# Pairing units product by product around a change of operands, and streaming the residual through DRAM, in a Strassen down projection

## The chip, the cores and the metric

The kernel runs on one core of a Trainium2 chip. The metric is the device time of one execution in microseconds (us), measured on the chip; the time before is the median of three runs. Beside the timed runs there is one profiled execution, whose trace gives the busy times, waits and transfers shown below. TensorE multiplies matrices, VectorE and ScalarE work element by element, SyncE (SP) and GpSimd (POOL) issue most of the DMA transfers.

## The reference

The reference is one inference step of a decoder layer, in float32, for a prompt of 512 tokens and 8 single decode tokens, which the kernel handles together as 520 columns. With D = 2048 and FF = 8192:

```
x = x + mixer(rmsnorm(x))                 # RG-LRU and mLSTM groups, projections w_in and w_out
x = x + cross_attn(rmsnorm(x), mk, mv)    # w_cq, w_mk, w_mv, w_co; 256 memory tokens
x = x + relu(rmsnorm(x) @ w_up)**2 @ w_down
y = rmsnorm(x) * g_final
```

It returns y for both kinds of tokens, the recurrent states, the convolution states, and the memory keys and values. The change is in the last matrix product, `@ w_down` (8192 x 2048), and in the helper that all the large products share.

## The kernel before

**Layout.** Activations lie transposed: 128 features on the partitions, 520 tokens in the free dimension, in two halves of 260 (`HT`). A float32 matrix is split into a high part and a low part, both in the fp32r type, and each product is three matmuls: high by high, high by low, low by high.

**Strassen products.** `strassen(key, n, ...)` computes a projection in `n` units of 256 output features. A unit is one level of Strassen's scheme in Winograd's form: seven products instead of eight. One product is 24 matmuls of 128 x 128 weights by 128 x 260 activations, accumulated in one PSUM bank; `ORDER` (L781) says for each product which of the three accumulators a, b, c it uses and which of the eight stored combinations of the activation blocks (a "slot") it reads. Accumulator a takes four of the seven products of a unit, c two, b one. `w_out`, `w_cq` and `w_co` have 8 units, `w_up` has 32. The 8192 rows of `w_down` are cut into four quarters, d0 to d3 (`NG = 4`), each with 8 units over the same 2048 outputs.

**Weights.** A unit reads four weight blocks of 128 x 1024 (A11, A21, A22, A12), fetched by `fetch` on SP's queue into a ring of seven tiles (`praw`, tag "raw"). `weights` (L877) forms the Strassen sums of the blocks on VectorE (L819), with one more tile of the ring for the running sum. `split_weights` (L97) makes the high part on ScalarE (L100) and the low part on VectorE (L101). In the main loop (L1428) weights are prepared two products ahead (`LOOK = 2`) and at a higher priority. A unit of the Strassen kind fetches the four blocks of the next unit during its first four products; the "plain" stages (keys and values of the memory) work in groups of four jobs, each with one weight block, and do the same.

**Operand sets.** For each projection the activations stand in DRAM as eight combinations (`td[key]`). Seven of them are in use, each as two batches of a high and a low tile: 28 tiles in the pool `ops`, all of its room. `set_load` (L848) loads one set: two transfers of 520 KB on SP's queue (L843), a cast on ScalarE (L844) and a subtraction on VectorE (L839) for each. A set of the next projection can be loaded only when the last unit of the current one has run the product that reads the old set in its place: `leave` is called after each product of the last unit. This happens between up and d0 and between the quarters of down.

**Evacuation.** After a product, `up_evac` copies or adds the accumulator into a tile t; after the seventh it squares the rectified result into w, forms the combinations and stores them to DRAM by POOL's queue (`spill`, L830). In down, `onto` (L927) adds the accumulator to the residual x on VectorE (L931). The residual is 16 tiles of 128 x 520, loaded at the start of d0 by `down_enter` (L1319) and kept in SBUF to the end, where `final` normalises and stores it.

**Order.** Pools and tiles come from a planner. It orders instructions by a priority, which follows the order of the program except that weights and evacuations are raised, and places the waits. Each engine and each DMA queue then works through its instructions in the planned order. `enter` closes the pools of a stage and opens those of the next in the same memory; a tile there waits for the tiles that held its place.

## Time and profile before

| | before |
|---|---|
| median of three runs | 2822.25 us |
| lowest and highest run | 2814.14 and 2824.98 us |
| the profiled execution, device time | 2829.93 us |
| its span, first to last instruction | 2828.2 us |
| TensorE busy | 2696.4 us, 95% |
| VectorE busy | 2265.6 us, 80% |
| ScalarE busy | 1389.7 us, 49% |
| moved by DMA | 525.67 MB, mean 186 GB/s |
| mean granted TensorE clock | 0.979 |

Up runs from about 1410 us of the span to about 2100, down from there to 2802. "Busy" is the time in which at least one instruction of an engine runs; matmuls overlap, so a busy TensorE need not be at its peak. The granted clock is the share of full speed that TensorE had. A line such as L839 is a line of the kernel, often in a helper that several stages use; then the names of the tiles tell the stage: op is an operand set, raw and raws are weight blocks, whi and wlo their high and low part, x the residual, acca, accb and accc the accumulators, tdd the DRAM copy of the operands of down. In a row of waits stand who waited and for whom, the total in us, how often, and the longest. In a row of windows stand the stretch in us, its length, the busy time of each engine with its number of instructions, the granted clock, the mean share of the DMA engines, and GB/s.

### The profile page before, as it was taken

To read this page: it belongs to the slowest core of one execution; us is meant where nothing else is said; L and a number is where in the kernel's file an instruction comes from. 1 tells how busy PE (TensorE), PEld (TensorE's weight loads), DVE (VectorE), ACT (ScalarE), POOL (GpSimd) and SP (SyncE) were. 2 spreads that over 40 slices of the span, in tenths; PEclk is the share of its full clock that TensorE was granted. 3 is DMA by queue.
4 is the path that set the end of the run, shared out by engine and by line. 5 is a ranking of instruction groups with operands and counts; after the bars stand their busy time and mean duration, and the time that the engine had idled before them with its cause. 6 is when DMAs were issued, how large, how long until landed. Compare 5 with 4: busy or idle time off the path is not lost.

```text
span 2828.2 us, 51905 instructions
## 1 busy us (share of the span) xinstructions
PE 2696.4 (95%) x21122; PEld 2613.9 (92%) x21122; DVE 2265.6 (80%) x3453; ACT 1389.7 (49%) x1857; POOL 93.9 (3%) x138
## 2 busy tenths in 40 slices
PE   8999999999999999989989999999999989999996
PEld 7999999999999997669979999999999989999896
DVE  7777787758888888789888777777787787887986
ACT  5455556535455444445464555555554343433543
POOL 0000000120000000000001000000000000000000
PEclk9999999999999999989999999999999999999998
DMA  4666542378677467985667454545465353533532
GB/s 167 191 216 212 191 151 91 115 272 271 203 260 261 158 197 282 328 300 188 207 214 262 150 166 150 166 150 165 150 210 203 105 191 102 172 126 112 191 107 82
DMA packets 173095, 525.67 MB, mean 186 GB/s; under 512 B 23084, under 2 KB 33004, under 8 KB 172856
## 3 DMA queue, kind: packets, MB, share of 16 engines
q1 hardware_dynamic: 151080, 442.50, 46.7%
q0 software_dynamic: 20624, 77.72, 7.8%
q8 instruction: 166, 2.72, 0.4%
q10 hardware_dynamic: 1152, 2.13, 0.2%
q14 instruction: 73, 0.60, 0.1%
HBM read 414.67 MB, written 107.73 MB: 185 GB/s over the span
## 4 chain that ended last, share of the span: by engine, by line
PE 74%; DVE 8%; DMA 7%; issue 7%; ACT 3%; POOL 0%; SPq 0%; DVEq 0%; POOLq 0%; ACTq 0%
PE acca L924 29%; PE accc L924 14%; PE mm L165 13%; PE accb L924 7%; PE mv L1159 3%; DVE wlo L101 2%; DVE op L839 2%; PE mk L1139 2%; PE ax L184 2%; DMA op<-tdd 2%; PE row L1086 1%; ACT whi L100 1%; DMA x<-dx 1%; PE aux L184 1%; ACT op L844 1%
## 5 line engine op out<-in xcount | busy, mean ns | idle before, releaser
L924 PE MATMUL acca<-op,whi 128*128 128x260 f32 x5632 | 1045.2, 285 | 37.9 <-DVE op L839 13.9
L924 PEld LDWEIGHTS acca<-op,whi 128*128 128x128 f32 x5632 | 876.6, 190 | 46.2 <-DVE op L839 17.7
L924 PE MATMUL acca<-op,wlo 128*128 128x260 f32 x2816 | 800.9, 284 | 4.5 <-DVE wlo L101 4.5
L100 ACT CAST whi<-raw 128x1024 fp32r<-128x1024 f32 x416 | 435.7, 1050 | 479.3 <-PE acca L924 155.2
L101 DVE TENSOR_TENSOR wlo<-raw,whi 128x1024 fp32r<-128x1024 f32 x416 | 506.8, 1220 | 73.7 <-ACT whi L100 69.0
L924 PEld LDWEIGHTS acca<-op,wlo 128*128 128x128 f32 x2816 | 534.5, 190 | 5.5 <-DVE wlo L101 5.2
L924 PE MATMUL accc<-op,whi 128*128 128x260 f32 x2816 | 523.2, 284 | 3.4 <-DVE op L839 1.8
L100 ACT CAST whi<-raws 128x1024 fp32r<-128x1024 f32 x264 | 276.8, 1049 | 399.7 <-PE accc L924 141.0
L165 PE MATMUL mm<-xa,whi 128*128 128x260 f32 x2624 | 433.3, 287 | 13.6 <-ACT whi L100 9.2
L924 PEld LDWEIGHTS accc<-op,whi 128*128 128x128 f32 x2816 | 437.0, 189 | 7.1 <-DVE op L839 2.9
L101 DVE TENSOR_TENSOR wlo<-raws,whi 128x1024 fp32r<-128x1024 f32 x264 | 322.5, 1222 | 124.7 <-ACT whi L100 124.2
L924 PE MATMUL accc<-op,wlo 128*128 128x260 f32 x1408 | 398.0, 283 | 0.0
L165 PEld LDWEIGHTS mm<-xa,whi 128*128 128x128 f32 x2624 | 367.4, 191 | 15.2 <-ACT whi L100 9.2
L924 PE MATMUL accb<-op,whi 128*128 128x260 f32 x1408 | 262.1, 285 | 15.6 <-DVE op L839 8.7
L165 PE MATMUL mm<-xa,wlo 128*128 128x260 f32 x1312 | 269.6, 287 | 0.0
L924 PEld LDWEIGHTS accc<-op,wlo 128*128 128x128 f32 x1408 | 266.4, 189 | 0.0
L924 PEld LDWEIGHTS accb<-op,whi 128*128 128x128 f32 x1408 | 218.2, 189 | 19.1 <-DVE op L839 11.0
L165 PEld LDWEIGHTS mm<-xa,wlo 128*128 128x128 f32 x1312 | 204.9, 191 | 0.5 <-DVE wlo L101 0.3
L924 PE MATMUL accb<-op,wlo 128*128 128x260 f32 x704 | 198.9, 282 | 0.0
L839 DVE TENSOR_TENSOR op<-op,op 128x1040 fp32r<-128x1040 f32 (+3 forms) x136 | 160.0, 1178 | 35.5 <-ACT op L844 26.3
L844 ACT CAST op<-op 128x1040 fp32r<-128x1040 f32 (+1 forms) x112 | 112.4, 1006 | 96.4 <-DMA op<-tdd 54.8
L100 ACT CAST whi<-wraw 128x1024 fp32r<-128x1024 f32 x82 | 85.6, 1044 | 142.9 <-PE mm L165 119.6
(367 smaller groups left out, 3232.0 us busy)
## 6 DMA issues: line engine op xcount, KB each, us to landing
raw<-in_w_up SPq DMA_DIRECT2D x128, 512.0 KB, 3.5
raw<-in_w_down SPq DMA_DIRECT2D x128, 512.0 KB, 3.5
wraw<-in_w_in SPq DMA_DIRECT2D x80, 512.0 KB, 4.5
tdd<-w POOLq DMA_DIRECT2D x32, 1040.0 KB, 6.3
op<-tdd SPq DMA_DIRECT2D x56, 520.0 KB, 5.5
raw<-in_w_mk SPq DMA_DIRECT2D x32, 512.0 KB, 5.1
raw<-in_w_out SPq DMA_DIRECT2D x32, 512.0 KB, 3.9
raw<-in_w_cq SPq DMA_DIRECT2D x32, 512.0 KB, 3.7
```

Of the source, the lines that this page charges most:

```text
L100: S.copy(hi, raw)
L101: V.tensor_tensor(out=lo, in0=raw, in1=hi.bitcast(F32), op=ALU.subtract)
L165: PE.matmul(ps[:, hf, 0:HT], w[:, j, :], x[:, HALF[hf]], start=(k == 0 and wi == 0), stop=(k == n - 1 and wi == 2))
L184: PE.matmul(out, u, v, start=first and i == 0, stop=last and i == 2)
L839: V.tensor_tensor(out=lo, in0=src, in1=hi.bitcast(F32), op=ALU.subtract)
L844: S.copy(hi[:, 0:n], lo[:, 0:n].bitcast(F32))
L924: PE.matmul(out, u[:, k], x[:, j], start=(new and k == 0 and i == 0), stop=(k == 7 and i == 2), skip_group_check=not new)
L1086: PE.matmul(ps, identr[0:NB, b:b + 1].to_broadcast([NB, P]), r, start=i == 0, stop=i == 1)
L1139: PE.matmul(st["mk"], u[:, i, :], x, start=(k == 0 and wi == 0), stop=(k == KB - 1 and wi == 2))
L1159: PE.matmul(st["mv"][i], x[:, ms], u[:, j], start=(k == 0 and wi == 0), stop=(k == KB - 1 and wi == 2))
```

## The change

The units around a change of operands run in pairs. `strassen` gets `pairs`: the first units of pairs. A pair runs product 0 of both units, then product 1 of both, and so on, so that both use the same operand set in turn. In d0, d1 and d2 units 0 and 1 and units 6 and 7 are pairs, in d3 units 0 and 1; up has none. The weights of the second unit of a pair (`seconds`) do not use the ring `praw`, but a pool y of four tiles, or tiles of the residual's pool in d3. Both units of a pair hold an accumulator a at the same time; there are two.

The main loop no longer fetches by the position in the unit before. Each weight block is fetched a fixed number of jobs before the job that first needs it (`NEED`): seven in a Strassen stage, four in a plain one.

The residual is no longer resident. `down_load(u)` loads the 128 x 1040 tile of unit u; in the first three quarters it is stored back to DRAM by POOL's queue after the unit's last product, with four tiles in the pool x; in d3 there are eight tiles and nothing is stored, so that `final` finds all of them. The loads are hung on products of earlier units (`hooks`, run at the end of a job). The pools of down are opened in the last unit of up, after its t and w have been allocated.

```diff
+YROW = 1154
...
             def go():
                 if "stack" in stage:
                     stage["stack"].close()
+                stage.clear()
                 stage["stack"] = ExitStack()
...
+        seconds = set()
+
         def fetch(k, q):
-            if k < len(sources):
+            if k not in seconds:
                 t = praw.tile([P, 8, P], F32, tag="raw", name=nm("raw"))
-                load(t, sources[k][q])
-                raws[k, q] = t
+            else:
+                n = "y" if "y" in stage else "x"
+                t = stage[n].tile([P, YROW] if n == "y" else [P, 2 * T], F32, tag=n, name=nm("rawp"))
+                t = t[:, 0:1024].rearrange("p (a b) -> p a b", b=P)
+            load(t, sources[k][q])
+            raws[k, q] = t
...
-        def strassen(key, n, src, evac, enter_=None, leave=None, left=None):
-
+        def strassen(key, n, src, evac, enter_=None, leave=None, left=None, pairs=(), hooks={}):
+            order = []
             for u in range(n):
-                k = len(sources)
-                sources.append([src(u, i, j) for i, j in ((0, 0), (1, 0), (1, 1), (0, 1))])
-                box = {}
-                for p in range(7):
-                    job = dict(unit=k, q=p, cost=0.3, prep=lambda k=k, p=p: weights(k, p),
...
+                if u in pairs:
+                    order += [(v, p) for p in range(7) for v in (u, u + 1)]
+                elif u - 1 not in pairs:
+                    order += [(u, p) for p in range(7)]
+            base, boxes = len(sources), [{} for _ in range(n)]
+            sources.extend([src(u, i, j) for i, j in ((0, 0), (1, 0), (1, 1), (0, 1))] for u in range(n))
+            seconds.update(base + u + 1 for u in pairs)
+            for u, p in order:
+                k, box = base + u, boxes[u]
+                job = dict(unit=k, q=p, kind=1, cost=0.3, prep=lambda k=k, p=p: weights(k, p),
...
+                if (u, p) in hooks:
+                    job["hook"] = hooks[u, p]
+                seq.append(job)
...
         def up_enter():
-            enter("d", t=2, w=2, x=2, r=1)()
+            enter("d", x=2, r=1, t=2, w=2)()
             start(scale_back())
...
         def up_evac(u, p, box):
             t = blocks(box, p)
+            if u == UP - 1 and p == 0:
+                box["w"] = tl("w", (P, 8, HT))
+                enter("e", y=4, x=4)()
             if p == 6:
-                w = tl("w", (P, 8, HT))
+                w = box.pop("w", None) or tl("w", (P, 8, HT))
...
-        def down_enter():
-            enter("e", x=16, ss=1)()
-            for m in range(KB):
-                X.append(tl("x", (P, T)))
-                load(X[m], dx[3][m // 2][:, m % 2])
+        def down_load(u):
+            x = tl("x", (P, 2 * T))
+            x = x.rearrange("p (i t) -> p i t", i=2)
+            load(x, dx[3][u])
+            X.append(x[:, 0])
+            X.append(x[:, 1])
+            st["X", u] = x
 
         def down_evac(u, p, box, last):
-            onto(X[2 * u:2 * u + 2], p, box["out"])
+            onto([st["X", u][:, 0], st["X", u][:, 1]], p, box["out"])
+            if p == 6 and not last:
+                store(dx[3][u], st["X", u])
...
-        strassen("up", UP, sq_src("w_up"), up_evac, up_enter, lambda s: set_load("d0", s))
+        strassen("up", UP, sq_src("w_up"), up_evac, up_enter, lambda s: set_load("d0", s),
+                 hooks={(UP - 1, 3): lambda: (down_load(0), down_load(1))})
+
+        def down_hooks(g):
+            last = g == NG - 1
+            hooks = {(1, 4): lambda: down_load(2)}
+            for u in range(2, 5):
+                hooks[u, 3] = lambda u=u: down_load(u + 1)
+            if last:
+                for u in (5, 6):
+                    hooks[u, 3] = lambda u=u: down_load(u + 1)
+            else:
+                hooks[5, 3] = lambda: (down_load(6), down_load(7))
+                if g == NG - 2:
+                    hooks[7, 3] = lambda: (enter("f", x=8, ss=1)(), X.clear())
+                    hooks[7, 5] = lambda: (down_load(0), down_load(1))
+                else:
+                    hooks[7, 3] = lambda: (down_load(0), down_load(1))
+            return hooks
+
         for g in range(NG):
+            last = g == NG - 1
             strassen(f"d{g}", 8, lambda u, i, j, g=g: a["w_down"][2 * u + i, g, j],
-                     lambda u, p, box, g=g: down_evac(u, p, box, g == NG - 1),
-                     down_enter if g == 0 else None,
-                     (lambda s, g=g: set_load(f"d{g + 1}", s)) if g < NG - 1 else None)
+                     lambda u, p, box, last=last: down_evac(u, p, box, last),
+                     leave=None if last else lambda s, g=g: set_load(f"d{g + 1}", s),
+                     pairs=(0,) if last else (0, 6),
+                     hooks=down_hooks(g))
...
-        for q in range(4):
-            fetch(0, q)
+        NEED = (0, 1, 1, 3)
+        fetches = [[] for _ in seq]
+        for n, j in enumerate(seq):
+            for i in range(4):
+                if j["q"] == (NEED[i] if j["kind"] else i):
+                    at = n - (7 if j["kind"] else 4)
+                    fetches[max(at, 0)].append((j["unit"], i, at < 0))
...
             with tc.high_priority(offset=AHEAD):
-                if j["q"] < 4:
-                    fetch(j["unit"] + 1, j["q"])
+                for k, i, early_ in fetches[n]:
+                    if not early_:
+                        fetch(k, i)
                 prep(n + LOOK)
...
+            if "hook" in j:
+                j["hook"]()
```

More of the change, by code (lines that the diff above doesn't have):

```diff
@@ L891, in weights @@
             return R((A11, SS, SS, A12, A21, SS, A22)[p])
[L893 removed]
+        def strassen(key, n, src, evac, enter_=None, leave=None, left=None, pairs=(), hooks={}):
+            order = []
             for u in range(n):
[L896 to L910 removed]
+                if u in pairs:
[8 more added lines that the diff above has]
+                job = dict(unit=k, q=p, kind=1, cost=0.3, prep=lambda k=k, p=p: weights(k, p),
+                           run=lambda w, p=p, box=box: product(key, p, w, box),
+                           post=lambda u=u, p=p, box=box: evac(u, p, box))
+                if u == 0 and p == 0 and enter_:
+                    job["enter"] = enter_
+                if u == n - 1:
+                    if leave:
+                        job["after"] = lambda p=p: leave(ORDER[p][2])
+                    if p == 6 and left:
+                        job["after"] = lambda p=p: (leave and leave(ORDER[p][2]), left())
+                if (u, p) in hooks:
+                    job["hook"] = hooks[u, p]
+                seq.append(job)
@@ L1374, in plain @@
                 for q in range(4):
-                    seq.append(dict(unit=k, q=q, cost=1.5, prep=lambda k=k, q=q: raws[k, q],
+                    seq.append(dict(unit=k, q=q, kind=0, cost=1.5, prep=lambda k=k, q=q: raws[k, q],
                                     run=lambda w, g=q0 + q: run(g, w), post=lambda g=q0 + q: post(g)))
@@ L1421, in rest @@
                 mem_load(k4, store)
-        for q in range(4):
-            fetch(0, q)
+        NEED = (0, 1, 1, 3)
[5 more added lines that the diff above has]
+                    fetches[max(at, 0)].append((j["unit"], i, at < 0))
+        for k, i, early_ in list(fetches[0]):
+            if early_:
+                fetch(k, i)
         for n in range(LOOK):
```

11 lines of the change are left out of this document (1 added, 10 removed).

## The prediction

> **What bounds the kernel now.** I read the page first, then the windows, the chain of waits, and the timelines of single engines, each time from a quiet stretch of the down projection to a change of operands.
>
> ```profile
> span 2828.2 us, 51905 instructions
> PE 2696.4 (95%) x21122; PEld 2613.9 (92%) x21122; DVE 2265.6 (80%) x3453; ACT 1389.7 (49%) x1857; POOL 93.9 (3%) x138
> ```
>
> TensorE is busy for 95% of the span, so only the rest, and matmuls at a lowered clock, can be won. Where does it lose time in down? The windows (us of the stretch, then busy time and instructions of each engine, clock, DMA share, GB/s) show a stretch inside a quarter, then the changes into the first, second and fourth quarter:
>
> ```profile
> 2145.00:2255.00 110.00, 110.00 (x916) 109.92 (x915) 88.93 (x102) 40.90 (x40) 0.00 (x0) 1.00 0.33 106
> 2080.00:2145.00 65.00, 53.35 (x410) 52.11 (x409) 52.08 (x57) 36.33 (x40) 1.70 (x2) 0.89 0.81 291
> 2255.00:2320.00 65.00, 57.65 (x436) 55.33 (x436) 52.70 (x58) 32.03 (x32) 0.00 (x0) 0.95 0.54 196
> 2605.00:2670.00 65.00, 58.63 (x469) 56.67 (x468) 56.82 (x65) 35.12 (x37) 0.00 (x0) 1.00 0.56 203
> ```
>
> Inside a quarter TensorE never stops. At the changes it idles 11.65, 7.35 and 6.37 us. What a change costs in all comes from the chain of waits (start, us, what): "x48" on acca is the last product of a unit followed by the first of the next, so it marks unit boundaries (x35 is the same piece cut short).
>
> ```profile
> 2082.71 5.77 PE acca L924 x48
> 2159.36 5.77 PE acca L924 x48
> 2179.56 5.77 PE acca L924 x48
> 2260.39 5.77 PE acca L924 x48
> 2333.81 5.77 PE acca L924 x48
> 2434.84 4.23 PE acca L924 x35
> 2507.94 5.77 PE acca L924 x48
> 2608.97 4.23 PE acca L924 x35
> 2678.50 5.77 PE acca L924 x48
> ```
>
> A quiet unit lasts 2179.56 - 2159.36 = 20.2 us, a product 2.887 us; 2159.36 to 2260.39 is five units without loss. Across each change lie three units (60.6 us), and the clock shows 76.65, 73.42, 73.10 and 69.53 us. So the changes cost 16.0, 12.8, 12.5 and 8.9 us: **50.2 us in all, the most that can be won here.**
>
> What is late in a change? The waits of TensorE at the first change, then VectorE back to back in the second (start, us, line, tile):
>
> ```profile
> PE acca L924 <- DVE x L931: 5.1, 1, 5.1
> PE accb L924 <- ACT op L844: 4.3, 1, 4.3
> PE accb L924 <- DVE op L839: 2.3, 2, 1.7
> ```
> ```profile
> 2289.85 1.22 DVE L101 TENSOR_TENSOR wlo<-raws,whi 128x1024 fp32r<-128x1024 f32 x1
> 2290.99 1.22 DVE L101 TENSOR_TENSOR wlo<-raw,whi 128x1024 fp32r<-128x1024 f32 x1
> 2292.12 0.42 DVE L931 TENSOR_TENSOR x<-accc,x 128x260 f32<-128x260 f32 x1
> 2292.46 1.22 DVE L101 TENSOR_TENSOR wlo<-raw,whi 128x1024 fp32r<-128x1024 f32 x1
> 2293.59 1.23 DVE L839 TENSOR_TENSOR op<-op,op 128x1040 fp32r<-128x1040 f32 x1
> 2294.74 0.42 DVE L931 TENSOR_TENSOR x<-acca,x 128x260 f32<-128x260 f32 x1
> ```
>
> When it never waits, VectorE starts a weight split (L101) every 1.14 us, a residual add (L931) every 0.34, an operand conversion (L839) every 1.15; the Strassen sums (L819, group row below) last as long as the splits. A unit has 7 splits, 7 adds and 4 sums: 14.9 us, **2.13 us per product of 2.887**.
>
> ```profile
> L819 DVE TENSOR_TENSOR raws<-raw,raws 128x1024 f32<-128x1024 f32 x33 | 40.3, 1222 | 0.7
> L819 DVE TENSOR_TENSOR w<-w 128x260 f32<-128x260 f32 x4 | 1.7, 423 | 0.0
> L819 DVE TENSOR_TENSOR w<-w 128x520 f32<-128x520 f32 x2 | 1.4, 694 | 0.0
> ```
>
> So VectorE has 0.76 us to spare per product, and a change adds 14 conversions, 16.1 us.
>
> **The change, part by part.**
>
> *Pairs at a change of operands.* Today the seven operand sets come free one per product in the last unit and are needed one per product in the next: set p free after product p, needed at 7+p. The first set is converted some three products in (5.5 us median to land, row below), the last is due at product 13. In those ten products VectorE must do 10 x 2.13 + 16.1 = 37.4 us in 28.9: 8.5 short. Weights are prepared two products ahead, which lets it slip about one product, 2.9 us: 5.6 us of stall by this sum against 7.35 and 6.37 in the windows, so the sum is usable. With pairs on both sides sets come free every second product and are needed every second one; the last is due at product 26 and conversions start about product 4: 22 products, 22 x 2.13 + 16.1 = 63.0 us in 63.5. It fits. If they run as they land, which the mixed order above suggests, twelve products carry one conversion each: 12 x (2.13 + 1.15 - 2.887) = 4.7 us too much, less 2.9 of slip: 1.8 us of stall. Lower end 0, upper end 1.8; I take 1.5, near the order shown. A stall cost 12.8/7.35 = 1.7 or 8.9/6.37 = 1.4 times its idle time, so I leave **2 us at each of the three changes between quarters: 34.2 - 6 = 28.2 us won.**
>
> *Into the first quarter* only the far side is paired, as up still ends with a single unit. Conversions run from product 3 to product 19: 16 x 2.13 + 16.1 + 1.5 (the three sums of up's last evacuation, 0.69 + 2 x 0.42 in the last two rows above) = 51.7 us in 46.2; 5.5 short, less 2.9: 2.6 us. Today's sum, to product 13, is 38.9 in 28.9, less 2.9: 7.1, plus the 5.1 us wait on x above: 12.2 against 11.65 measured.
>
> *That wait on x* is the residual. Today sixteen loads stand in SP's queue at this change, for memory that up's last tiles still hold:
>
> ```profile
> 2117.46 0.85 POOL L830 DMA_DIRECT2D tdd<-w  x1 [23.21 <-ACT op L844]
> 2120.56 8.21 SPq L1319 DMA_DIRECT2D x<-dx  x3
> ```
>
> Three issues took 8.21 us, beginning behind the spill of up's last tile, and every load behind them on SP waited. Afterwards two loads stand there, asked for three products earlier, but the memory of the new stage still overlaps up's last t and w. In a pair, product 2 of the same unit comes four products later instead of two, so an add may be later before TensorE waits. Between 0 and 5.1 us, then; I take 2.5. Idle 2.6 + 2.5 = 5.1, times 16.0/11.65: 7 us stay, **9 us won.**
>
> *The residual through DRAM.* The issues (KB each, median us to landing) that price it, x<-dx and dx<-x being the same kind of tile in other stages:
>
> ```profile
> raw<-in_w_down SPq DMA_DIRECT2D x128, 512.0 KB, 3.5
> op<-tdd SPq DMA_DIRECT2D x56, 520.0 KB, 5.5
> x<-dx SPq DMA_DIRECT2D x24, 520.0 KB, 6.4
> dx<-x POOLq DMA_DIRECT2D x24, 520.0 KB, 4.9
> ```
>
> 32 loads replace 16 half-sized ones, and 24 stores are new. A load is asked for after product 3 and used at the end of product 0 of the next unit, 4 x 2.887 = 11.5 us later; it needs 6.4. A store lies on POOL's queue, empty in down but for spills, and has more than two units (40 us) before its buffer is loaded again; it needs 4.9. Traffic: 1.06 MB per 20.2 us, 53 GB/s on top of the 106 of the quiet window; at a change the paired units spread the sets' 7.45 MB over 80 us. I cost it at **0**, hidden by the unit before; uncovered, it is rival three.
>
> *Loads of weights by need.* The second units' weights go into their own ring; the load of A22 there waits on SP for a split one or two products away (up to 5.8 us), with set loads and residual loads behind it. The sets have 12 products of time: 0. Elsewhere A22 is fetched a product earlier (0), and where a plain stage follows Strassen units its first weights come four products ahead instead of seven:
>
> ```profile
> DMA to landing us min/median/max: 6.1/7.2/10.0
> PE acca L924 <- ACT whi L100: 1.4, 1, 1.4
> ```
>
> The first row is the mv weights: with preparation two products ahead 5.8 us remain, so 0.3 to 4.2 us could be late. The second is the wait at the start of out that goes when Strassen weights come seven ahead instead of four. From -1.4 to +4.2; I take 0, since the slip of a product covers the median.
>
> *The clock.* Two windows and the longest waits (total, times, longest) of the second change, one window of the fourth:
>
> ```profile
> 2305.00:2310.00 5.00, 4.25 (x21) 3.75 (x20) 3.17 (x4) 3.11 (x4) 0.00 (x0) 0.56 0.90 333
> 2310.00:2315.00 5.00, 5.00 (x35) 5.00 (x34) 0.87 (x2) 0.96 (x2) 0.00 (x0) 0.76 0.01 6
> PE acca L924 <- DVE op L839: 3.0, 2, 2.0
> 2650.00:2655.00 5.00, 2.36 (x15) 1.94 (x16) 3.32 (x5) 2.11 (x2) 0.00 (x0) 1.00 0.99 374
> ```
>
> Much the same stalls lowered the clock to 0.56 once and not at all the other time; the difference, 12.8 - 8.9 = 3.9 us, is what it costs, and is in my ratio. The Trainium skill ("TensorE: Matmul & The Clock Gate", HAM oscillation) has the clock fall after idle gaps of over some 3.4 us; the longest wait in the second change is 2.0 us, so the trace disagrees. By that rule the short stalls I leave would cost their idle time alone, 3 x 1.5 + 5.1 = 10 us instead of 13, and the forecast would be 2782.
>
> **Sum.** 28.2 + 9 = 37.2 us won. The profiled execution took 2829.93 us (span 2828.2): 2792.7 after. It lies 7.7 us above the median of the three runs, 2822.25, so against the median the forecast is **2785 us**. Half a per cent, 14 us, is about what a measurement of this kernel can tell from no change.
>
> **Rivals.**
> 1. *VectorE keeps half of the bound.* Conversions jam the first pair, the slip is used up, each stall lowers the clock: 4.7 us of idle at 1.7 is 8 us per change between quarters and 8 more into the first, and the wait on x stays (5.1): 37 left, 13.2 won: **2809**. For it: VectorE's fit is within 0.5 us; against: twice the time for the same work.
> 2. *The pairing doesn't reach the bound*, because sets are late by their transfers (TensorE's 4.3 us on ACT's op above) and not by when they come free. Then each change costs what it did: **2822**. Against: DMA share 0.54 and 0.56 at the later changes.
> 3. *Slower: the residual comes late.* If a load of x stands behind a waiting issue of 8.21 us and needs 6.4 more with 3.5 for a weight load before it, it takes 18.1 us; 11.5 and one product of slack cover 14.4, so VectorE, with the splits queued behind the add, holds TensorE 3.7 us in each such unit. In all 18 single units: 66.6 - 37.2 = 29 slower, **2852**. It decides from (37.2 + 14)/3.7 = 14 units on. Against: in quiet units nothing on SP waits for long and landings are 6.4 us.
>
> **How the numbers follow.** Forecast 0.70 (its own range 2772, with nothing left at the changes, to 2796, with the high ends of stall, x and mv: 3 x 1.8 x 1.7 + 7.7 x 1.4 + 4.2 = 24 left), first rival 0.17, second 0.07, third 0.06. The range 2770 to 2810 leaves out the last two and a little. Faster by over 0.5% (below 2808): the forecast and half of the first rival, 0.79; within 0.5%: half the first and most of the second, 0.15; slower 0.06.
>
> **What would show it.** Right: unit boundaries of 20.2 us across the changes between quarters within 2 to 3 us; L839 gone from TensorE's waits; VectorE near 5.00 per 5 us for some 60 us, not 30; the first change still the dearest; clock 1.00 at the later three. Wrong: VectorE waiting on x<-dx inside a quarter (third rival), L101 or L839 still holding TensorE for over 4 us a change (first), conversions waiting for op<-tdd as before (second).

## The result, and the profile after

| | before | changed kernel |
|---|---|---|
| median | 2822.25 us (5 runs, 2814.14 to 2827.66) | 2803.39 us (5 runs, 2802.3 to 2807.62) |
| ratio to before, 95% interval | | 0.9929 [0.9911, 0.9947] |
| span of the profiled execution | 2828.2 us | 2805.8 us |
| down, from the start of up's last Relu to the end of the span | 719.5 us | 697.0 us |
| the four changes of operands | 50.2 us | 26.3 us |
| co to up, as measured below | 78.8 us | 87.9 us |

The kernel became 0.7% faster: 18.9 us by the medians and 22.4 us by the profiled spans, where 37.2 were forecast. The forecast time, 2785 us, is 18 us too low; its range, 2770 to 2810, holds the result, but the range that the forecast gave itself without its rivals, 2772 to 2796, does not. One of the ten runs of the kernel fetch_only below took 3700.84 us at a granted clock of 0.657 and counts in its median, while the ratios compare fast runs alone.

The page of the changed kernel, the same two lines as shown of before:

```profile
span 2805.8 us, 52010 instructions
PE 2689.8 (96%) x21122; PEld 2612.2 (93%) x21122; DVE 2263.9 (81%) x3453; ACT 1389.2 (50%) x1857; POOL 106.9 (4%) x162
```

TensorE runs as many matmuls as before and is busy 6.6 us less; the rest of the gain is idle time. In this kernel's line numbers the matmuls of the products are L942, the set loads L845, their cast and rest L846 and L841, the splits of weights L101 and L102, the residual add L949, the residual's loads L1339 and stores L1347, weight loads L876. Its windows (a stretch inside a quarter, the change into the first, the second and the fourth quarter, then five microseconds of the second; columns as before):

```profile
2180.00:2250.00 70.00, 70.00 (x585) 70.00 (x585) 57.52 (x66) 25.55 (x25) 2.14 (x4) 1.00 0.48 155
2085.00:2150.00 65.00, 59.48 (x450) 58.04 (x449) 55.28 (x61) 37.38 (x41) 1.70 (x2) 0.92 0.77 279
2255.00:2320.00 65.00, 61.33 (x482) 60.35 (x481) 56.95 (x64) 32.75 (x33) 1.07 (x2) 0.95 0.64 224
2605.00:2670.00 65.00, 62.73 (x507) 62.32 (x506) 57.10 (x69) 31.82 (x36) 1.07 (x2) 0.97 0.62 219
2300.00:2305.00 5.00, 4.80 (x19) 4.20 (x20) 5.00 (x7) 3.84 (x4) 0.00 (x0) 0.50 0.53 213
```

TensorE's idle time at these changes fell from 11.65, 7.35 and 6.37 us to 5.5, 3.7 and 2.3. It is not gone, and the clock still falls, to 0.50 in the second change. The chain of waits of the changed kernel gives what a change costs (start, us, what; each row is the end of a unit, the first of up's last but one):

```profile
2085.31 5.78 PE acca L942 x48
2177.94 5.78 PE acca L942 x48
2198.10 5.78 PE acca L942 x48
2218.27 5.78 PE acca L942 x48
2346.73 5.78 PE acca L942 x48
2387.06 5.78 PE acca L942 x48
2510.56 5.78 PE acca L942 x48
2550.90 5.78 PE acca L942 x48
2676.30 5.78 PE acca L942 x48
```

A quiet unit takes 20.17 us (2198.10 to 2218.27). From 2085.31 to 2177.94 lie four units, so the change into the first quarter costs 92.63 - 80.67 = 12.0 us; between the later pairs of rows lie six units each (121.0 us): 128.46, 123.50 and 125.40 us, so 7.5, 2.5 and 4.4 us. Forecast were 7, 2, 2 and 2.

**Where the rest went.** The way from co to up, which the change also touches, became dearer. I measure it from ScalarE's square of co's last but one unit to the Relu of up's second unit, and down from the Relu of up's last unit; the rows of ScalarE's timeline, before and then after:

```profile
1416.99 1.06 ACT L970 ACTIVATE sq<-x 128x1040 f32<-128x1040 f32 x1
1495.78 1.08 ACT L1308 ACTIVATE t<-t 128x1040 f32<-128x1040 f32 x1
2108.72 1.07 ACT L1308 ACTIVATE t<-t 128x1040 f32<-128x1040 f32 x1
```
```profile
1411.84 1.06 ACT L988 ACTIVATE sq<-x 128x1040 f32<-128x1040 f32 x1
1499.74 1.07 ACT L1329 ACTIVATE t<-t 128x1040 f32<-128x1040 f32 x1
2108.82 1.07 ACT L1329 ACTIVATE t<-t 128x1040 f32<-128x1040 f32 x1
```

Down won 719.5 - 697.0 = 22.5 us. From co to up 78.8 us became 87.9. The remaining 9.0 us of the 22.4 by which the span fell (22.5 - 9.1 + 9.0) lie ahead of co's end and inside up. That the changed kernel is 5.2 us earlier at the end of co isn't to be read as a gain: in the nine kernels below that are written the same up to this point the first of these rows lies between 1407.06 and 1416.86 us. The down figure, on the other hand, repeats: two kernels that differ only in how early weight blocks are asked for have 719.5 and 719.5, two others 757.1 and 757.4, and three have 697.0, 697.0 and 697.3. In the last of these (need_two) the single changes moved and only their sum stayed, so part of that agreement is chance, and no kernel was profiled twice. I take differences of a few microseconds in down as real; this is a judgement and not a measured error.

### The profile page after: what moved, and what is told of

The parts are those of the page before. It is cut to its first block, busy times and chain, and to the rows that moved or that the text cites. A ratio compares the mean times of both kernels' runs of the same rounds, so it can differ in the third digit from the quotient of the medians.

```text
span 2805.8 us, 52010 instructions
## 1 busy us (share of the span) xinstructions
PE 2689.8 (96%) x21122; PEld 2612.2 (93%) x21122; DVE 2263.9 (81%) x3453; ACT 1389.2 (50%) x1857; POOL 106.9 (4%) x162
## 4 chain that ended last, share of the span: by engine, by line
PE 80%; DMA 8%; DVE 6%; ACT 3%; issue 2%; SPq 0%; DVEq 0%; ACTq 0%
PE acca L942 33%; PE accc L942 16%; PE mm L166 12%; PE accb L942 9%; PE mv L1177 3%; PE mk L1157 2%; DVE wlo L102 1%; PE ax L185 1%; DMA op<-tdd 1%; PE row L1104 1%; DVE op L841 1%; PE aux L185 1%; ACT whi L101 1%; DMA ct<-in_C 1%; ACT op L846 1%
## 5 line engine op out<-in xcount | busy, mean ns | idle before, releaser
L942 PE MATMUL acca<-op,whi 128*128 128x260 f32 x5632 | 1042.8, 285 | 30.7 <-ACT t L960 11.9
L942 PEld LDWEIGHTS acca<-op,whi 128*128 128x128 f32 x5632 | 877.6, 190 | 35.6 <-ACT t L960 12.9
L942 PE MATMUL acca<-op,wlo 128*128 128x260 f32 x2816 | 802.7, 285 | 4.3 <-DVE wlo L102 4.2
L101 ACT CAST whi<-raw 128x1024 fp32r<-128x1024 f32 x388 | 406.8, 1050 | 441.9 <-PE acca L942 142.7
L942 PEld LDWEIGHTS acca<-op,wlo 128*128 128x128 f32 x2816 | 536.2, 190 | 6.3 <-DVE wlo L102 6.3
L102 DVE TENSOR_TENSOR wlo<-raw,whi 128x1024 fp32r<-128x1024 f32 x388 | 473.0, 1220 | 64.6 <-ACT whi L101 61.0
L942 PE MATMUL accc<-op,whi 128*128 128x260 f32 x2816 | 515.3, 282 | 1.4 <-DVE op L841 0.9
L101 ACT CAST whi<-raws 128x1024 fp32r<-128x1024 f32 x264 | 277.0, 1049 | 385.8 <-PE accc L942 111.5
L942 PEld LDWEIGHTS accc<-op,whi 128*128 128x128 f32 x2816 | 434.6, 188 | 3.8 <-issue 1.5
L102 DVE TENSOR_TENSOR wlo<-raws,whi 128x1024 fp32r<-128x1024 f32 x264 | 322.7, 1222 | 119.7 <-ACT whi L101 119.0
L942 PE MATMUL accc<-op,wlo 128*128 128x260 f32 x1408 | 397.2, 282 | 0.0
L942 PE MATMUL accb<-op,whi 128*128 128x260 f32 x1408 | 260.8, 285 | 8.1 <-ACT op L846 4.6
L942 PEld LDWEIGHTS accc<-op,wlo 128*128 128x128 f32 x1408 | 265.3, 188 | 0.0
L942 PEld LDWEIGHTS accb<-op,whi 128*128 128x128 f32 x1408 | 218.9, 190 | 9.5 <-ACT op L846 4.8
L942 PE MATMUL accb<-op,wlo 128*128 128x260 f32 x704 | 199.3, 283 | 0.0
L841 DVE TENSOR_TENSOR op<-op,op 128x1040 fp32r<-128x1040 f32 (+3 forms) x136 | 159.9, 1179 | 37.6 <-ACT op L846 26.7
L846 ACT CAST op<-op 128x1040 fp32r<-128x1040 f32 (+1 forms) x112 | 112.2, 1006 | 96.6 <-DMA op<-tdd 51.3
L101 ACT CAST whi<-wraw 128x1024 fp32r<-128x1024 f32 x82 | 85.6, 1044 | 140.3 <-PE mm L166 116.7
```

Of the source, the lines that this page charges most:

```text
L101: S.copy(hi, raw)
L102: V.tensor_tensor(out=lo, in0=raw, in1=hi.bitcast(F32), op=ALU.subtract)
L841: V.tensor_tensor(out=lo, in0=src, in1=hi.bitcast(F32), op=ALU.subtract)
L846: S.copy(hi[:, 0:n], lo[:, 0:n].bitcast(F32))
L942: PE.matmul(out, u[:, k], x[:, j], start=(new and k == 0 and i == 0), stop=(k == 7 and i == 2), skip_group_check=not new)
```

## The experiments

All with their medians, ratios to before with the 95% interval, and the two stretches. The four columns on the right are the costs of the changes where the chain shows them; for d_order_back, layout and need_two they are read from TensorE's timeline, from the starts of the last products of the same units. Spans and costs come from one profiled execution of each kernel.

| kernel | median us | ratio | co to up | down | d0 | d1 | d2 | d3 |
|---|---|---|---|---|---|---|---|---|
| before | 2822.25 | | 78.8 | 719.5 | 16.0 | 12.8 | 12.5 | 8.9 |
| changed | 2803.39 | 0.9929 [0.9911, 0.9947] | 87.9 | 697.0 | 12.0 | 7.5 | 2.5 | 4.4 |
| no_pairs | 2869.53 | 1.0154 [1.0132, 1.0177] | 88.8 | 757.1 | 22.5 | 23.8 | 22.9 | 19.2 |
| fetch_only | 2825.75 | 0.9994 [0.9980, 1.0007] | 81.2 | 719.5 | | | | |
| stream_only | 2866.62 | 1.0151 [1.0123, 1.0179] | 88.6 | 757.4 | | | | |
| tied_single | 2842.98 | 1.0065 [1.0043, 1.0087] | 87.7 | 731.0 | 16.4 | 13.6 | 14.9 | 18.6 |
| tied | 2801.29 | 0.9915 [0.9894, 0.9935] | 88.0 | 691.3 | 11.4 | 2.2 | 1.4 | 5.9 |
| no_store | 2795.19 | 0.9893 [0.9867, 0.9919] | 90.6 | 685.7 | 9.9 | 2.5 | 1.0 | 2.2 |
| x_pool | 2820.78 | 0.9977 [0.9964, 0.9991] | 90.8 | 712.7 | 16.2 | 7.8 | 8.6 | 9.7 |
| late_cast | 2803.70 | 0.9924 [0.9899, 0.9949] | 89.0 | 693.8 | 15.4 | 0.1 | 0.1 | 7.4 |
| d_order_back | 2796.09 | 0.9898 [0.9875, 0.9922] | 81.2 | 697.0 | 12.4 | 6.5 | 2.8 | 4.7 |
| layout | 2797.31 | 0.9899 [0.9875, 0.9922] | 81.4 | 690.5 | 7.5 | 4.4 | 3.3 | 4.6 |
| need_two | 2809.45 | 0.9945 [0.9928, 0.9961] | 90.8 | 697.3 | 12.1 | 3.1 | 3.1 | 7.1 |
| best | 2790.97 | 0.9893 [0.9872, 0.9914] | 79.7 | 687.6 | 13.9 | 0.1 | 0.1 | 3.2 |

### 1. What the pairs are worth

```diff
-                     pairs=(0,) if last else (0, 6),
+                     pairs=(),
```

> The changed kernel with no units in pairs in down; the residual still streams through DRAM, weights are still loaded by need. Theory (pairs give what was won at the changes between quarters, streaming costs nothing): these changes go back to 12.8, 12.5 and 8.9 us from 7.5, 2.5 and 4.4, and the change into the first quarter to between 12 and 16: 20 to 24 us slower than the changed kernel, 2823 to 2827 us. Rival A (a part of the gain comes from the streaming or the earlier weights): 2805 to 2815 us. Rival B (streaming costs time that pairs hide): over 2832 us, with waits on x<-dx in single units.

Slower than the changed kernel by 66 us and slower than before by 1.5%. Each change costs more than it did before: 88.4 us in all against 50.2. That is rival B in size, but without its sign: TensorE's waits are not on the residual inside a quarter. They are on sets that are late; its two longest rows in down:

```profile
PE accb L942 <- ACT op L846: 14.0, 4, 4.1
PE acca L942 <- ACT op L846: 13.4, 8, 2.5
```

The pairs are thus worth 757.1 - 697.0 = 60 us, more than the 50.2 that I took for all that can be won, and some other part of the change costs 38 us without them.

### 2. Which part costs 38 us

Two kernels take the rest apart: the fetch by need alone, put into the kernel before, and the streaming without it.

```diff
+        NEED = (0, 1, 1, 3)
...
-                if j["q"] < 4:
-                    fetch(j["unit"] + 1, j["q"])
+                for k, i, early_ in fetches[n]:
+                    if not early_:
+                        fetch(k, i)
```

> The kernel before with one part of the change alone: weights are loaded by need (A22 in the same product as A21; a plain stage's four products ahead), no pairs, the residual held in SBUF. Down is measured from the end of up's last Relu to the end of the span: 719.5 us before, 697.0 in the changed kernel, 757.1 without its pairs. Theory N (two weight loads in one product find too few free buffers, SP stands before them and the sets queue behind, which is what made the kernel without pairs 44 us slower than before): down takes 740 to 757 us, the time is 2840 to 2860 us. Rival S (the streaming does that, by residual loads on SP that wait 103 us for stores): down stays at 719.5 within 4 us, and the way from mv to co gets 5.5 us shorter: 2813 to 2822 us.

```diff
-                     pairs=(0,) if last else (0, 6),
+                     pairs=(),
...
-        NEED = (0, 1, 1, 3)
+        NEED = (0, 1, 2, 3)
```

> The changed kernel without pairs and with A22 loaded one product after A21 as before: streaming, the new order of memory and the later first weights of plain stages remain. Theory N: down is back at 719.5 us within 5, the time 2824 to 2834 us (before, and up to 9 for the way from co to up). Rival S (streaming costs it): down stays at 750 to 760 us, the time at 2860 to 2872 us.

Rival S, twice: down takes 719.5 us with the fetch alone and 757.4 with the streaming alone. The fetch by need changes nothing that can be measured, 0.9994 [0.9980, 1.0007], with a median 4 us above rival S's range and far from N's; that it shortens the way from mv to co, which I had read from one execution, is not confirmed. The residual through DRAM, which I had costed at nothing, costs 37.9 us in the kernel without pairs (with it the new places of the pools in memory, which no run takes apart there).

### 3. How the streaming costs it

SP's timeline at the change into the second quarter in the kernel without pairs, and SP's waits in the stretch from 2250 to 2350 us of that kernel:

```profile
2301.36 0.86 SPq L845 DMA_DIRECT2D op<-tdd  x2
2310.47 0.32 SPq L1339 DMA_DIRECT2D x<-dx  x1
2310.89 0.37 SPq L876 DMA_DIRECT2D raw<-in_w_down  x1
2311.35 0.38 SPq L845 DMA_DIRECT2D op<-tdd  x1
```
```profile
SPq L1339 <- DMA dx<-x: 23.0, 4, 8.2
```

Between two loads of sets stands one load of the residual, for unit 3 of the next quarter. The program asks for it in unit 2. But in the planned order it stands earlier, as soon as its memory comes free, and that is the tile that unit 7 of the old quarter has just sent to DRAM. SP stands until that store has landed, up to 8.2 us, and the sets behind it wait along. The Trainium skill ("DMA: Bandwidth & Descriptors", Anatomy of one DMA — SWDGE (gpsimd) path) says, in a section on GpSimd's path, that DMA engines do not wait for semaphores and that any such wait happens on the issuing sequencer before the DMA is dispatched; the gap on SP from 2302.22 to 2310.47 agrees with that. The test ties the residual's load to its place in the program, behind the last weight load asked for before it:

```diff
-            load(t, sources[k][q])
+            st["last"] = load(t, sources[k][q]).ins
...
-            load(x, dx[3][u])
+            with tc.issue_after(st["last"]):
+                load(x, dx[3][u])
```

> The changed kernel without pairs, in which each load of the residual in down is issued on SP behind the last weight load asked for before it in the program; without that, loads of units 2 and 3 of the next quarter stand on SP between the loads of the sets, before buffers that the stores of units 6 and 7 still hold. Traffic and loads are the same. Theory W (SP's standing before those loads delays the sets): down, 757.1 us without pairs, comes back to 718 to 728 us, the time to 2826 to 2838 us, and SP's waits on dx<-x fall from 103 us to under 30. Rival T (the residual's traffic itself delays the sets): down stays over 745 us, the time over 2855 us.

Down comes from 757.1 to 731.0 us with the same transfers; 3 us above the range that theory W gave for down (5 for the time), and far from rival T. SP's wait on dx<-x is gone. So 26 of the 38 us hung on the place of these loads in SP's list. The tie takes away SP's standing and also moves the loads' own transfers, 520 KB each, away from the sets'; it doesn't tell the two apart. Of the 11.5 us that stay against before, 9.7 lie at the last change (18.6 against 8.9), where the stage's memory is opened anew. TensorE waits for sets again there (9.1 us in four rows); why these sets are late is not shown, since the cause that experiment 5 finds, the place of second units' weights, does not exist without pairs.

> The changed kernel, pairs and all, with the same tie of the residual's loads. Theory W: the four changes, 26.3 us, come to 12 to 18 us, down to 683 to 690 us, the time to 2789 to 2797 us. Rival (in pairs the sets have time enough, and SP's standing costs nothing any more; what is left is ScalarE's order and the place of the second units' weights): down stays at 697 within 3 us, the time at 2800 to 2806 us.

With pairs the same tie wins 5.7 us of down (691.3), 1.3 above theory W's range; the second change falls from 7.5 to 2.2 us, the third from 2.5 to 1.4. The four changes come to 20.9 us, where theory W had 12 to 18. The time lies in the rival's range, and by it alone, 0.9915 [0.9894, 0.9935], this kernel can't be told from the changed one. The mechanism is the same in the changed kernel, at a lower price. POOL's timeline, SP's, ScalarE's and TensorE's at its second change:

```profile
2281.27 0.53 POOL L1347 DMA_DIRECT2D dx<-x  x1 [38.65 <-DVE x L949]
2285.03 0.53 POOL L1347 DMA_DIRECT2D dx<-x  x1 [3.22 <-DVE x L949]
```
```profile
2278.47 0.38 SPq L845 DMA_DIRECT2D op<-tdd  x1
2284.38 0.32 SPq L1339 DMA_DIRECT2D x<-dx  x1
2284.80 0.38 SPq L845 DMA_DIRECT2D op<-tdd  x1
2292.93 0.32 SPq L1339 DMA_DIRECT2D x<-dx  x1
2293.34 0.38 SPq L845 DMA_DIRECT2D op<-tdd  x1
```
```profile
2290.25 1.06 ACT L846 CAST op<-op 128x1040 fp32r<-128x1040 f32 x1 [4.68 <-DMA op<-tdd]
2291.22 1.05 ACT L101 CAST whi<-raws 128x1024 fp32r<-128x1024 f32 x1
2297.82 1.06 ACT L846 CAST op<-op 128x1040 fp32r<-128x1040 f32 x1 [5.55 <-DMA op<-tdd]
2298.78 1.04 ACT L101 CAST whi<-raws 128x1024 fp32r<-128x1024 f32 x1
```
```profile
2299.88 0.80 PE L942 MATMUL acca<-op,whi 128*128 128x260 f32 x2 [3.18 <-ACT whi L101]
```

Read across the four: the residual of unit 7 goes out at 2285.03; SP stands from 2285.18 until it has landed, 2292.93; the set behind it is asked for at 2293.34; ScalarE stands 5.55 us before that set's cast; the weight cast that it does next, at 2298.78, is what TensorE has waited 3.18 us for. The set itself isn't urgent. It holds up weights which are, because their cast stands behind its cast in ScalarE's list.

### 4. ScalarE's order

This kernel leaves SP as it is and cuts the story one step later: the conversions of down's sets stand four products behind their loads.

```diff
+        def set_late(key, s, n):
+            for b in range(2):
+                hi, lo = op_tile(), op_tile()
+                load(lo.bitcast(F32), td[key][b][:, s])
+                sets.setdefault((key, s), []).append((hi, lo))
+                later.setdefault(n + 4, []).append((hi, lo))
...
+            for hi, lo in later.pop(n, []):
+                S.copy(hi, lo.bitcast(F32))
+                lo_of(lo, lo.bitcast(F32), hi)
             j["run"](ws.pop(n))
```

> The changed kernel with the same loads of down's sets at the same places, but the conversions of a set (ScalarE's cast and VectorE's rest) placed four products after its load. Theory (ScalarE takes its list in order and stands before a cast whose transfer hasn't landed, up to 6.3 us, while casts of weights for the next product queue behind it): the waits of ScalarE for op<-tdd fall from 51.3 us in all to under 10, TensorE's waits for splits of weights at the changes go, and the changes between quarters cost under 2 us each: 8 to 14 us faster, 2789 to 2795 us. Rival (VectorE's work is the bound, not ScalarE's order): later conversions press it into fewer products, and the time is 2800 to 2812 us, with waits on L841's conversions coming back.

At the second and third change the theory holds to the letter: 0.1 us each, 7.5 and 2.5 in the changed kernel, and ScalarE has no wait for op<-tdd left. The window of the second change in this kernel:

```profile
2255.00:2320.00 65.00, 65.00 (x544) 65.00 (x543) 64.45 (x72) 36.55 (x37) 1.07 (x2) 1.00 0.75 270
```

TensorE is busy throughout at full clock, with VectorE at 64.45 of 65 us: the pair just fits VectorE, as the prediction's sum (63.0 us of work in 63.5) had it. At the first and the last change the cost rose instead, from 12.0 to 15.4 and from 4.4 to 7.4 us, so that down wins only 3.2 us and the time is unchanged: rival by the time, though without its sign, since TensorE waits for no conversion; theory by two changes of four. What is late at those two is not a set: the chain goes through the second unit's weights (rawp) at the last, and at the first TensorE waits 7.1 us for the cast of such a block, before which ScalarE stands 4.54 us for its transfer.

### 5. The last change, and the residual's stores

```diff
             onto([st["X", u][:, 0], st["X", u][:, 1]], p, box["out"])
-            if p == 6 and not last:
-                store(dx[3][u], st["X", u])
```

> The changed kernel with the residual's loads tied behind weight loads, and with the 24 stores of the residual in down left out: each quarter then adds to the residual as it stood after up, so the sums of the quarters are not carried on; loads, sets, weights and pairs are as they were. With the stores in, the four changes cost 11.4, 2.2, 1.4 and 5.9 us and down 691.3. Theory M (what is left at the change into the last quarter is SP standing 8.3 us before second units' weights whose memory is a residual tile still being stored): that change comes to 1 to 3 us, the first stays at 10 to 13 us, since nothing is stored there, and down comes to 686 to 689 us. Rival T (the traffic of the stores delays all transfers of a quarter): all three later changes go to 0 to 1 us, and down to 683 to 686 us. Rival Z (neither): down stays at 691.3 within 2 us.

The last change falls from 5.9 to 2.2 us, the two in the middle stay (2.5 and 1.0), the first is 9.9: theory M by the changes, with 1.5 us less at the first that it didn't foresee. Down, 685.7, lies 0.3 us under its range and so in rival T's, but T wanted all three later changes at 0 to 1. In the tied kernel SP's waits from 2570 to 2640 us show what the stores did there:

```profile
SPq L876 <- DMA dx<-x: 8.3, 2, 7.0
```

For the last quarter eight residual tiles take the memory of the second units' weights and of the four old ones, and the second unit's weights of its first pair are put where a residual is still on its way to DRAM. SP stands before the second and third weight load of that unit. Their sum is needed by the unit's second product, the fourth of the quarter, and TensorE waits there 0.81 and 0.94 us for its split; it waits 1.75 us for the unit's first block too, which was asked for at 2601.59, before SP stood. At the other two changes the traffic of the stores costs nothing that shows.

### 6. The residual's loads on another queue

```diff
-            load(x, dx[3][u])
+            store(x, dx[3][u])
```

> The changed kernel, with the loads of the residual in down issued by POOL instead of SP; nothing else moves. Theory (SP is blocked): in the changed kernel SP stood 80.2 us, in 15 waits, before a residual load whose store had not landed, and 10.5 us behind the spill of up's last tile; the set loads and weight loads queued behind. Without that the change into the first quarter should cost about 7 us instead of 12.0, and the three changes between quarters about 9 instead of 14.4 in all: 2793 us, with no wait on dx<-x left on SP. Rival (ScalarE waits in order for the sets' own transfers, whatever SP does): each change keeps its cost within 1.5 us, 2800 to 2806 us.

Neither. The wait went with the loads to POOL, as hoped, and SP has none on a residual load left; yet down grew by 15.7 us, with three of the changes dearer and the second the same (7.8 us). SP's waits in down before weight loads, first of the changed kernel and then of this one:

```profile
SPq L876 <- DVE raws L821: 207.2, 39, 8.8
SPq L876 <- DVE wlo L102: 124.9, 37, 12.7
```
```profile
SPq L876 <- DVE raws L821: 252.1, 37, 15.0
SPq L876 <- DVE wlo L102: 196.4, 49, 12.2
```

With the residual's loads gone from SP, the planner laid SP's list anew, and SP stands 116 us longer before weight loads whose ring has no free tile. That alone is no explanation, since the kernel before has as much of it (262.2 and 178.9 us). At the second change the picture is the one of experiment 3 with another load in front: ScalarE stands 5.81 us before the cast of a set, and TensorE 3.85 us for a weight cast behind it; the set was asked for from 2299.25 on, behind a weight load before which SP stood for up to 10.4 us. So taking this one wait off SP was not enough. Why the other changes are dearer stays open.

### 7. The order of memory in up's stage

```diff
-            enter("d", x=2, r=1, t=2, w=2)()
+            enter("d", t=2, w=2, x=2, r=1)()
```

> The changed kernel with the memory of up's stage in the old order (t, w, x, r). Theory (the new order lays up's first t tile on co's w tiles, so its copy comes later in ScalarE's list, behind seven casts of sets): TensorE's wait of 10.0 us on t at the change from co to up goes back to about 2 us, and the way from co to up costs 8.8 us less; the second units' first weights of down then lie on up's last t and w, so the change into the first quarter grows by 0 to 5 us. Sum 2795 to 2800 us. Rival (the 8.8 us come from weights fetched by need or from chance): the wait on t stays near 10 us, and the time is 2803 us or more.

0.9898 [0.9875, 0.9922], 7 us below the changed kernel by the medians, and from co to up 81.2 us instead of 87.9. TensorE's waits from 1440 to 1480 us in the changed kernel, and from 1400 to 1480 in this one:

```profile
PE acca L942 <- ACT t L960: 10.3, 2, 10.0
```
```profile
PE acca L942 <- ACT t L960: 1.7, 1, 1.7
```

The nine kernels with the new order have 87.7 to 90.8 us for this way, the mean is 89.1; the five in which t lies on co's x tiles have 78.8 to 81.4, mean 80.5. So the new order costs 8.7 us. With it the first copy into t stands sixteen places later in ScalarE's list, behind casts of sets that wait for transfers: the same kind of order as in experiment 4. For down the new order was worth nothing: 697.0 us with either. So this part of the change gives 8.7 us away for nothing.

### 8. Where the second unit's weights lie, and how early they are asked for

```diff
-YROW = 1154
+YROW = 1040
...
-            enter("d", x=2, r=1, t=2, w=2)()
+            enter("d", t=2, x=2, r=1, w=2)()
```

> The changed kernel with other places in memory: up's stage in the order t, x, r, w, and rows of 1040 instead of 1154 numbers for the second units' weights. Then up's t tiles lie on co's x tiles as before the change, and of the first four weights of down's second unit only the last lies on up's last t. Theory (at the change into the first quarter SP stands 13.7 us before weights whose memory is up's last t; from co to up t comes late by its place): from co to up 11 to 14 us less, as with the old order alone, and the change into the first quarter costs 5 to 8 us instead of 12.0: 2786 to 2792 us, down 690 to 693 us. Rival (something else is late there, such as the residual behind the spill of up's last tile, 10.5 us): down stays at 697 within 2 us, the time at that of the old order, 2794 to 2799 us.

In the spans the theory holds: from co to up 81.4 us, down 690.5. The time, 0.9899 [0.9875, 0.9922], falls to the rival's 2794 to 2799; with 6.5 instead of 11 to 14 us from co to up, the theory's sum was too large. The change into the first quarter costs 7.5 us, inside the theory's 5 to 8, and the second 4.4 instead of 7.5. But the theory's reason isn't borne out: SP still stands 12.80 us before the second unit's four weight blocks at the change into the first quarter, where it stood 13.70. What differs is how many of them go out late. In the changed kernel three leave at 2111.02, just before the spill of up's last tile, which takes 9.8 us to land; here only the last block leaves then, and the spill lands after 7.0 us. So the residual's load and the set behind it follow earlier, and the second stop of TensorE at this change (see "Into the first quarter" below) is gone. That the three loads slow the spill is argued from these two traces and not tested; why the second change is cheaper is open.

> The changed kernel with A22 loaded one product of its own unit later, so no two weight loads of a unit fall on one product. Theory N: SP stands less before weight loads and the sets come earlier; the four changes, 26.3 us, lose 3 to 12 us: 2791 to 2800 us, down 685 to 694 us. Rival S: in pairs A22 is then five products ahead of its use instead of seven, which is enough, and nothing is won: 2800 to 2808 us, down 697 us within 4; if the way from mv to co loses its 5.5 us too, 2809 us.

The edit is the line `NEED = (0, 1, 2, 3)` alone. Down 697.3 us: nothing in sum, though the second change fell from 7.5 to 3.1 us and the last rose from 4.4 to 7.1. The time, 2809.45 us, is the figure that rival S gave for the case that mv to co loses 5.5 us, but 2.9 of the 6 us above the changed kernel lie between co and up, and the intervals overlap. With experiment 2 the fetch by need is out as a cause of what down loses or wins in sum.

### 9. Three edits together

The places of experiment 8, the late conversions of 4, the tie of 3.

> The changed kernel with three edits together: the other places in memory (t on co's x, second units' weights off up's last t), conversions of down's sets four products after their loads, the residual's loads tied behind weight loads. If the three remove different waits, down comes to 680 to 686 us (697.0, less 6.5 and 3.2 as measured for the first two alone, less 2 to 8 for the tie) and the time to 2780 to 2790 us. If they remove the same waits, down stays at 688 to 692 us and the time at 2793 to 2799 us, as with the places alone.

0.9893 [0.9872, 0.9914], 2790.97 us: the fastest by the median of all that compute the whole, 12 us below the changed kernel, though each is measured beside its own runs of before and the two intervals still overlap. In down it is between the two cases, 687.6. The two middle changes cost 0.1 us each, the last 3.2. Most of what is left, 13.9 us, is the change into the first quarter, with one long wait (TensorE's waits from 2077 to 2175 us; then ScalarE's row):

```profile
PE acca L951 <- ACT whi L101: 6.9, 1, 6.9
```
```profile
2108.63 1.04 ACT L101 CAST whi<-rawp 128x1024 fp32r<-128x1024 f32 x1 [4.31 <-DMA rawp<-in_w_down]
```

The weights of the second unit (rawp) land too late. They are asked for only at 2098.12, two microseconds before up's last evacuation, behind nine set loads in SP's list. That this is the cause is not tested: no run here asks for them earlier with the late casts.

## Why the prediction was half right, step by step

That the range holds the result is in part luck: it does so because it reached over the first rival's 2809, to which 2803.39 is nearer than to the forecast's 2785. What the runs show for the time that stayed, sets and weights that come late through the lists of SP and ScalarE, is in neither the forecast nor that rival.

**What bounds the changes.** Right: pairs take the bound off, and VectorE then just fits. The late-cast kernel shows it at two changes; at the second TensorE is busy for 65 of 65 us and VectorE for 64.45. The first rival (VectorE keeps half of the bound) falls with that row, and its sign is missing in the changed kernel: VectorE's splits (L102) hold TensorE for 3.8 us in all of down, its conversions (L841) not at all. That VectorE was the bound before is read from the trace, where it works without a break from 2286.07 to 2304.63 us; pairs give the transfers twice the time as well, and no run tells the two apart.

**Pairs, "2 us at each of the three changes".** Too low: 7.5, 2.5 and 4.4 us stayed, 8.4 more than the 6 forecast. What stayed was not the stall of conversions that I had worked out. TensorE no longer waits for a conversion (L841) at these changes but for splits of weights. At the second change they wait behind casts of late sets (experiments 3 and 4). At the last, second units' weights wait for memory (experiment 5, in the kernel with the tie). I had looked at the work of an engine per product, not at the order in which it is done.

**"The residual through DRAM: cost 0".** This is the step that failed. I compared 4.9 us for a store with "more than two units (40 us)" until its buffer is loaded again. By the hooks it is 8 to 18 products, 23 to 52 us, so the figure was too high for some units; but even the shortest is far above 4.9 us, and that isn't what failed. The order that runs is another: the load stands right behind the store, on SP. Alone, the streaming costs 37.9 us; with pairs, the tie and the left-out stores together win 697.0 - 685.7 = 11.3 us back, and that is about what the sum lacked in down, 37.2 - 22.5 = 14.7. My third rival had the mechanism, a residual load in SP's line, and the wrong place and victim. It priced every single unit at 3.7 us through the residual's add; inside a quarter nothing was lost (the chain shows 20.17 us a unit), and what suffered were the sets behind the load, at the changes. Without pairs the kernel would have been on that rival's side: 2869.53 us, where before had 2825.58 beside it.

**"Into the first quarter 7 us stay".** 12.0. The wait on x of 5.1 us is gone, as forecast, and TensorE waits for no conversion. It stops twice, until 2113.90 (2.65 us) and until 2131.37 (1.37 us), each time for the cast of a weight block (TensorE's waits from 2085 to 2150 us, then SP's rows and ScalarE's):

```profile
PE acca L942 <- ACT whi L101: 4.0, 2, 2.6
```
```profile
2098.60 13.70 SPq L876 DMA_DIRECT2D rawp<-in_w_down  x4
2112.96 11.46 SPq L1339 DMA_DIRECT2D x<-dx  x2
2124.53 0.38 SPq L845 DMA_DIRECT2D op<-tdd  x1
```
```profile
2129.31 1.06 ACT L846 CAST op<-op 128x1040 fp32r<-128x1040 f32 x1 [6.26 <-DMA op<-tdd]
```

The first stop ends with the second unit's first block. It was asked for at 2098.60, but its cast starts at 2112.81, behind up's last evacuation and two casts of sets. The second stop ends with a weight cast behind a set's cast, which stood 6.26 us for its transfer; that set was asked for at 2124.53, behind the residual's load, before which SP stood for the spill of up's last tile (11.46 us for the two loads). I had priced the overlap with up's t and w for the add that uses the residual, and not for the set that stands behind its load. The other three blocks wait for that memory too, but TensorE doesn't wait for them here.

**Weights by need: 0.** Right for the sum, 0.9994 [0.9980, 1.0007].

**What I did not cost.** The new order of pools in up's stage stands in the diff, and I read it as a matter of down. It lost 8.7 us between co and up. Of the 18 us between forecast and result this is the term that no step of mine had.

**The clock.** Right in kind. Idle time of 3.7 us at the second change (65 less 61.33) cost 7.5, and the five microseconds after it ran at 0.50. The longest single wait there is 3.18 us. The rule of the Trainium skill ("TensorE: Matmul & The Clock Gate", HAM oscillation), which has the clock fall after gaps of over some 3.4 us, is again not what this trace shows, though 3.18 lies near it; the kernel before, with 0.56 behind waits of at most 2.0 us, speaks more clearly. Of the marks that I set, L841 left TensorE's waits and the first change is still the dearest; unit boundaries within 2 to 3 us came true for one change only, the clock was 0.95 and 0.97, not 1.00, at the second and the fourth, and VectorE was busy for 56.95 of 65 us at the second, not throughout.

## What to carry to other kernels

A load that is costless by its own arithmetic can still stand in the line of others: when a buffer goes out and comes in again, look where the planned order puts the load on its queue and what stands behind it, not where the program asks for it. On an engine that takes its list in order, work that isn't urgent but waits for a transfer must stand behind urgent work that doesn't. And every line of a diff that moves memory has a stage before it and one after it; both have to be costed.

## What was not expected of the hardware

How steady a stretch is and how unsteady its start: down agrees within 0.4 us between kernels with the same work there (with the reserve made above), while the time at which co's last unit but one ends scatters by 9.8 us between kernels that are written the same up to there. A gain of 5 us read from two traces at one place, as mine from mv to co, says nothing until another execution of the same part has been seen.

A store of 520 KB issued at 2285.03 let SP go on at 2292.93, 7.9 us later, where the median landing of these stores is 4.8 us: the store that matters ran at a change, beside the loads of the sets (DMA share 0.86 from 2285 to 2290 us).
